# Four transformer layers on one core: plain float32 matmuls in place of three products of 12-bit parts

## The chip, the core and the metric

The kernel runs on one core of a Trainium2 chip. The metric is the device time of one execution in microseconds (us). The engines of the core are named as in the profile: PE is the tensor engine (PEld its weight loads), DVE the vector engine, ACT the scalar engine, POOL GpSimd, SP the engine whose queue issues most transfers. Each engine works through its own list of instructions in order and waits on semaphores.

## What is computed

One inference step of a diffusion backbone with 1024 features, for 512 latent tokens and 128 prompt tokens, 640 in all. There are four layers, each with another kind of attention over 16 heads (neighbourhood attention; a sliding window with grouped keys; latent attention of low rank with a rotary part; grouped keys with rotary positions). Everything is float32.

```python
for li in range(DEPTH):                                  # DEPTH = 4
    hp = modulate(rms_norm(xp, norm1_g[li]), mp[0], mp[1])   # prompt, 128 tokens
    hs = modulate(rms_norm(xs, norm1_g[li]), ms[0], ms[1])   # latents, 512 tokens
    ...                                                  # q, k, v; softmax(q k + bias) v; w_o
    x = x + gate * heads_out(o, w_o)
    h = modulate(rms_norm(x, norm2_g[li]), ...)
    x = x + gate * ((silu(h @ w_gate) * (h @ w_up)) @ w_down)   # 2816 hidden features
```

## The kernel before

A layer L has two stages. The attention stage makes the normalised and modulated activations (`make_h`), then the token-major products for queries, keys and values (`proj_first`, `proj`; for layer 2 `products_q` and `products_k`), normalises the heads, transposes queries and keys on PE, and goes through 16 units, each a pair of heads and a half of the latents: scores into PSUM tiles `S`, softmax, transposes of the weights into `tp`, the product with the values into `sm` (tiles `pt` and `v`). Between these, generators of other work are advanced a step at a time (`job`, `tick`): the next group's products, its preparation, a half of the output product, the next layer's modulation. The feed-forward stage (`rest`) finishes the output product, normalises again (`make_b`), and forms gate and up with seven block products in place of eight (`gate_up`: quarters of the weights and of the activations, and sums of such quarters named S1 to S4 and T1 to T4), then the product down. Feature-major products have 320 columns (half of the 640 tokens) and accumulate in tiles `big`.

Every linear product is made from parts: a float32 block of weights `raw` or `sum` is copied to a 12-bit high part `whi` on ACT (line 309, type float32r), and the rest `wlo` is the difference, on DVE or POOL (line 310). Activations are cut likewise into `hh` and `hl`, attention outputs and hidden features into `ah` and `al`. A product is then three matmuls: high by high, high by low, low by high (`mm3`, `feat`, `block`; all matmuls are recorded at line 269, in `mm`).

Scores use the array's 128 rows for 64 features: a head's queries stand as high part above low part (`stack`), its keys' high part is doubled into both halves of the rows, and so is the low part (`double`, by a transfer); two matmuls give the score, in layer 2 a third one adds the rotary part (tiles `qpe`, `kpe`).

The order of the instructions on each engine comes from a scheduler that a model of the time drives; blocks of attention have priority. Weight blocks have 4 places each for `raw`, `whi` and `wlo`, in the feed-forward stage 4, 9 and 9, and 4 for `sum`.

Some products are plain float32 already: the sums of squares against ones (tiles `t` and `consts`), the modulation (`raw`, `rawm` with `cond`, four products of 32 columns side by side in the array), the product with the values (two heads of 64 columns side by side).

Of the kernel before, what the change touches and what calls it, by code (L numbers as in the profile page):

```python
# [9 lines left out]
F32R = mybir.dt.float32r  # L10
# [4 lines left out]
P = 128  # L15
D = 1024
ND = 8
# [27 lines left out]
# ---------------------------------------------------------------- layout of the weights  # L45
# [5 lines left out]
def weight_plan():  # L51
    """(key, features tiles, columns, builder) of every weight of a product, in the order of use."""
# [59 lines left out]
# columns (one value a partition) and rows (one value a column, the same in every partition)  # L112
# [55 lines left out]
def to_perm(a):  # L168
    """Latent tokens from (row, column) order to (column // 8, row, column % 8) order, first axis."""
    return a.reshape(8, 8, 8, *a.shape[1:]).swapaxes(0, 1).reshape(a.shape)  # L170


def host_arrays(a):
# [54 lines left out]
    h["ck0"] = kdup(a["cache_na_k"], np.arange(HD))  # L228
# [31 lines left out]
# ---------------------------------------------------------------- the kernel  # L260
class Net:
    def __init__(self, nc, tc, a, o, depth=DEPTH):
        self.nc, self.tc, self.a, self.o, self.depth = nc, tc, a, o, depth
        self.flip, self.flop = 0, 0
        self.slots(None)

    # -- small helpers
# [3 lines left out]
    def alt(self, out, in_, share=0.5):  # L271
        """A copy, on the scalar engine for a share of the calls and on the vector engine for the others."""
        self.flip += share
        if self.flip >= 1:
            self.flip -= 1
            self.nc.scalar.copy(out, in_)
        else:
            self.nc.vector.tensor_copy(out, in_)

    def banks(self, kind):  # L280
        """The accumulators of a phase: name -> (banks of each, number)."""
# [8 lines left out]
    def weights(self, key, part=None):  # L290
        """The blocks of a weight, or one of them, on chip in two parts: for each feature tile (high, low) [128, n]."""
        i, k, n, per = WIDX[key]
        nc, out = self.nc, []
        for j, k0 in enumerate(range(0, k, per)):
# [4 lines left out]
            nc.sync.dma_start(raw[:, :w], self.a["wall"][i + j, :, :w])  # L299
            self.flop += 0 if self.more else 1  # L300
# [12 lines left out]
    def slots(self, more):  # L313
        """The places of blocks and of their parts, in turn; the feed-forward phase has some more of them."""
        self.more = more
        self.free = {n: [f"{n}{i}" for i in range(SLOTS)] for n in ("raw", "whi", "wlo")}
# [4 lines left out]
    def slot(self, name):  # L321
# [3 lines left out]
        return pool.tile([P, BLK], F32 if name in ("raw", "sum") else F32R, tag=tag, name=name)  # L325
# [12 lines left out]
    # -- the whole  # L338
# [38 lines left out]
    # -- modulation: silu(cond) @ w_mod + b_mod, as columns  # L377
# [6 lines left out]
    def mod_first(self, b, pool):  # L384
        """The first layer's shift and scale of feature tiles 2 b and 2 b + 1."""
# [22 lines left out]
    def mod_part(self, L, c0, w, pool, tag=None, bufs=1):  # L408
        """Columns c0 to c0 + 4 w - 1 of the layer's modulation: four products side by side in the array."""
# [32 lines left out]
    def fill(self, n):  # L442
        """n steps of the work that waits for idle time of the tensor engine."""
# [46 lines left out]
    def new_act(self):  # L490
        hi = self.cp.tile([P, T], F32R, tag="hh", name="hh", bufs=ND)
        lo = self.cp.tile([P, T], F32R, tag="hl", name="hl", bufs=ND)
        return hi, lo

    def make_h(self, pool, L, n, ds=range(ND), src=None):
# [3 lines left out]
        for d in ds:  # L499
            hi, lo = self.new_act()  # L500
            u = pool.tile([P, T], F32, tag="u", name="u", bufs=2)
            for c, (c0, c1) in enumerate(((0, NL), (NL, T))):
                s = src[d] if src is not None and c == 0 else self.x[:, d, c0:c1]
                nc.vector.scalar_tensor_tensor(u[:, c0:c1], s, moda[:, n, d, c:c + 1], self.rstd[:, c0:c1],
                                               ALU.mult, ALU.mult)
            for c, (c0, c1) in enumerate(((0, NL), (NL, T))):
                nc.scalar.activation(hi[:, c0:c1], u[:, c0:c1], AF.Identity, bias=self.mcol(L, 3 * n, d, c))
            for c, (c0, c1) in enumerate(((0, NL), (NL, T))):
                nc.vector.scalar_tensor_tensor(lo[:, c0:c1], u[:, c0:c1], self.mcol(L, 3 * n, d, c),
                                               hi.bitcast(F32)[:, c0:c1], ALU.add, ALU.subtract)  # L510
            self.h.append((hi, lo))

    # -- products
    def mm3(self, out, x, w, start, stop):
        """out += x.T @ w to float32's accuracy, from parts of 12 bits."""
        self.mm(out, x[0], w[0], start, False)
        self.mm(out, x[0], w[1], False, False)
        self.mm(out, x[1], w[0], False, stop)

    def proj_first(self, key, n, evac):  # L520
        """Token-major product of h, the features outermost: five accumulators of n columns."""
# [5 lines left out]
        for k, w in enumerate(self.weights(key)):  # L527
            hh, hl = self.h[k]
            for t in range(NTT):
                ts = slice(t * P, (t + 1) * P)  # L530
                self.mm3(acc[t], (hh[:, ts], hl[:, ts]), w, k == 0, k == ND - 1)
# [3 lines left out]
    def proj(self, key, n, evac):  # L535
        """Token-major product of h, a step for each tile of tokens."""
        ws = self.weights(key)
        for t in range(NTT):
            ts = slice(t * P, (t + 1) * P)
            acc = self.ps()[:, :n]  # L540
            for k in range(ND):
                hh, hl = self.h[k]
                self.mm3(acc, (hh[:, ts], hl[:, ts]), ws[k], k == 0, k == ND - 1)
# [28 lines left out]
    def residual(self, L, i, d, halves):  # L572
        """x += gate * y for one feature tile of y, or a half of it: halves is {half: y}."""
# [6 lines left out]
    # -- products by seven block products (Strassen, Winograd's form)  # L580
# [3 lines left out]
    def scaled(self, pool, L, halves, d, raws):  # L584
        """A feature tile of x (or a half of it) by its scale, for make_b."""
        nc = self.nc
        if d not in raws:
            raws[d] = pool.tile([P, T], F32, tag="a", name="raw", bufs=12)
# [10 lines left out]
    def make_b(self, pool, L, B, raws):  # L599
        """The second normalisation: the quarters of h that the seven block products take and their sums, all in two  # L600
        parts: B[name] = [(high, low) of feature tile i of the half's four]. A step for each feature tile of the first
        half of the tokens, and one for the rest. The latents' shift joins the quarters and sums when they are split."""
        nc = self.nc
        lo, hi = slice(0, 320), slice(320, T)
        t3 = [pool.tile([P, 2, 320], F32, tag="a", name="raw", bufs=12) for _ in range(HALF // 2)]
        slots = [self.new_act() for _ in range(ND)]
        for tag, w in (("c", T), ("d", 320)):
            slots += [[pool.tile([P, w], F32R, tag=x + tag, name=x, bufs=HALF) for x in ("hh", "hl")] for _ in range(HALF)]
        shift = self.mods[L][0][:, 24:24 + ND]
        more = pool.tile([P, ND + HALF], F32, tag="more", name="more")  # L610
        self.sub(nc.gpsimd, more[:, :ND], shift[:, :, 1], shift[:, :, 0])
        self.sub(nc.gpsimd, more[:, ND:], shift[:, HALF:, 0], shift[:, :HALF, 0])

        done = []
# [1118 lines left out]
```

## Time and profile before

| | |
|---|---|
| time, median of 3 runs | 3288.86 us (3283.66 to 3291.21) |
| span of the profiled execution | 3285.3 us |
| busy: PE, PEld, DVE, ACT, POOL | 3123.6, 2847.0, 2155.9, 1527.9, 1264.1 us |
| matmul records | 22157 |
| mean granted clock of PE | 0.979 of 2.4 GHz |

The span runs from the first to the last instruction of one profiled execution; for it no other time than the span is at hand, and it lies within the runs'. Busy time is the union of an engine's instructions. The chip records a plain float32 matmul as two instructions and one of type float32r as one; both are shown as f32.

### The profile page before, as it was taken

Reading aid. Unit: us, or ns where it says so; the run is one execution under the profiler, and the core shown is the slowest. Engines: PE = TensorE matmul, PEld = TensorE weight load, DVE = VectorE, ACT = ScalarE, POOL = GpSimd, SP = SyncE. Lnnn points to the kernel's source line nnn. Section 1 sums busy time; section 2 is a strip of 40 time slices with the busy share of each in tenths; the row PEclk is TensorE's granted clock in tenths of the full one; section 3 lists DMA queues with packets and bytes.
Section 4 is the critical chain, followed back from the end, with each engine's and each line's share of the span. In section 5 each row is a group of like instructions: output and inputs, shape, how many; then the busy total and the mean of one; then the engine's idle time right before and its main releaser. Section 6 shows DMA issues by size and latency. Waiting matters only on the chain. (4 is left out here: it accounts for less than half of the span.)

```text
span 3285.3 us, 58663 instructions
## 1 busy us (share of the span) xinstructions
PE 3123.6 (95%) x22157; PEld 2847.0 (87%) x22157; DVE 2155.9 (66%) x4167; ACT 1527.9 (47%) x3300; POOL 1264.1 (38%) x1175
## 2 busy tenths in 40 slices
PE   8999989999999999999987999999999999899999
PEld 6997879999887788999976778899998878799999
DVE  5554496666576768667668766865765765867665
ACT  4555453433346755334346765433433576534332
POOL 2442362322244444323234545432322553633322
PEclk9998999999999999999998999999999999899999
DMA  7346542433433343222211223423333111122222
GB/s 236 100 119 195 184 155 86 127 104 117 126 122 98 105 135 105 76 84 83 88 45 40 64 64 120 135 86 119 117 102 122 53 32 29 55 87 76 80 82 83
DMA packets 168251, 331.50 MB, mean 101 GB/s; under 512 B 19616, under 2 KB 49696, under 8 KB 167968
## 3 DMA queue, kind: packets, MB, share of 16 engines
q1 hardware_dynamic: 164800, 323.47, 32.6%
q8 instruction: 175, 2.87, 0.4%
q10 hardware_dynamic: 3168, 4.28, 0.4%
q14 instruction: 108, 0.88, 0.1%
HBM read 303.86 MB, written 4.28 MB: 94 GB/s over the span
## 5 line engine op out<-in xcount | busy, mean ns | idle before, releaser
L269 PE MATMUL big<-hh,whi 128*128 128x320 f32 x2720 | 829.9, 315 | 24.7 <-ACT hh L619 8.5
L269 PE MATMUL big<-hl,whi 128*128 128x320 f32 x2720 | 832.1, 312 | 6.7 <-DVE hl L623 4.6
L269 PE MATMUL big<-hh,wlo 128*128 128x320 f32 x2720 | 824.1, 311 | 0.9 <-DVE wlo L310 0.9
L309 ACT CAST whi<-raw 128x512 fp32r<-128x512 f32 (+3 forms) x668 | 387.7, 586 | 674.1 <-PE big L269 431.8
L310 DVE TENSOR_TENSOR wlo<-raw,whi 128x512 fp32r<-128x512 f32 (+1 forms) x504 | 432.5, 862 | 201.6 <-ACT whi L309 198.5
L269 PEld LDWEIGHTS big<-hh,whi 128*128 128x128 f32 x2720 | 508.4, 190 | 53.9 <-DVE sv L696 13.6
L269 PEld LDWEIGHTS big<-hl,whi 128*128 128x128 f32 x2720 | 511.7, 190 | 20.9 <-DVE hl L623 10.8
L269 PEld LDWEIGHTS big<-hh,wlo 128*128 128x128 f32 x2720 | 510.1, 189 | 2.9 <-DVE wlo L310 2.9
L310 DVE TENSOR_TENSOR wlo<-sum,whi 128x512 fp32r<-128x512 f32 x336 | 302.0, 903 | 73.3 <-ACT whi L309 68.4
L309 ACT CAST whi<-sum 128x512 fp32r<-128x512 f32 x352 | 215.8, 618 | 272.5 <-PE big L269 226.4
L269 PE MATMUL big<-al,whi 128*128 128x320 f32 x1408 | 335.9, 311 | 3.2 <-POOL al L582 3.2
L310 POOL TENSOR_TENSOR wlo<-raw,whi 128x512 fp32r<-128x512 f32 (+2 forms) x164 | 223.4, 1374 | 294.4 <-ACT whi L309 266.5
L269 PE MATMUL big<-ah,whi 128*128 128x320 f32 x1408 | 333.8, 312 | 1.2 <-ACT ah L734 1.2
L269 PE MATMUL big<-ah,wlo 128*128 128x320 f32 x1408 | 333.4, 310 | 0.0
L1018 POOL TENSOR_SCALAR p<-p,st 128x640 f32<-128x640 f32 (+2 forms) x256 | 201.2, 790 | 315.7 <-DVE st L1017 227.9
L709 POOL TENSOR_TENSOR y<-y,sv 128x320 f32<-128x320 f32 x132 | 146.7, 1118 | 354.0 <-DVE sv L696 300.8
L670 POOL TENSOR_TENSOR sum<-raw,sum 128x512 f32<-128x512 f32 x88 | 124.0, 1409 | 410.1 <-ACT whi L309 206.2
L670 POOL TENSOR_TENSOR sum<-raw 128x512 f32<-128x512 f32 x88 | 127.5, 1449 | 364.7 <-DMA raw<-in_wall 180.6
L577 DVE SCALAR_TENSOR_TENSOR x<-big,mod,x 128x320 f32<-128x320 f32 (+2 forms) x480 | 182.4, 432 | 117.4 <-PE big L269 116.8
L269 PEld LDWEIGHTS big<-al,whi 128*128 128x128 f32 x1408 | 240.2, 189 | 6.5 <-POOL al L582 3.7
L269 PEld LDWEIGHTS big<-ah,whi 128*128 128x128 f32 x1408 | 238.3, 188 | 8.0 <-issue 2.5
L269 PEld LDWEIGHTS big<-ah,wlo 128*128 128x128 f32 x1408 | 239.6, 189 | 0.2
(264 smaller groups left out, 6169.2 us busy)
## 6 DMA issues: line engine op xcount, KB each, us to landing
raw<-in_wall SPq DMA_DIRECT2D x644, 256.0 KB, 2.7
rawm<-in_wmod SPq DMA_DIRECT2D x144, 512.0 KB, 4.3
raw<-in_wmod SPq DMA_DIRECT2D x96, 256.0 KB, 4.5
k<-k SPq DMA_DIRECT2D x38, 384.0 KB, 4.4
raw<-in_wall SPq DMA_DIRECT2D x96, 128.0 KB, 2.2
bias<-in_nabias SPq DMA_DIRECT2D x16, 576.0 KB, 5.5
qpe<-pes SPq DMA_DIRECT2D x56, 80.0 KB, 2.1
out_y<-x ACTq DMA_DIRECT2D x8, 320.0 KB, 2.2
```

The source lines that it names most:

```text
L269: self.nc.tensor.matmul(out, lhsT=lhsT, rhs=rhs, start=start, stop=stop, skip_group_check=True)
L309: self.nc.scalar.copy(hi, raw)
L310: eng.tensor_tensor(lo, raw, hi.bitcast(F32), ALU.subtract)
L577: self.last = self.nc.vector.scalar_tensor_tensor(xs, halves[b][:, p0:p1], self.mcol(L, i, d, c), xs, ALU.mult, ALU.add)
L670: eng.tensor_tensor(raw[n], raw[x], raw[y], op)
L709: nc.gpsimd.tensor_tensor(y, y, v, ALU.mult)
L1018: nc.gpsimd.tensor_scalar(p, p, rd, 1.0, ALU.mult, ALU.mult)
```

## The change

All cuts into parts go, and with them `two`, `stack`, `split`, `double`, `o_split`, `acts`, `first_group` and `spread`. A linear product is one plain float32 matmul on the block and the activation as they are. A pair of heads has one tile of queries and one of keys, 64 rows for each head (where four heads share a key it stands in both halves, doubled before the transpose); a score is one matmul on 64 rows, and in layer 2 a second one on the 32 rows of the rotary part. Weight blocks get 12 places, in the feed-forward stage 20, sums 8. In `make_b` the normalised quarters are used in place and the sums are made from them. Attention outputs get tiles of their own (`oo`).

```diff
-SLOTS = 4
-MORE = {"whi": 5, "wlo": 5, "sum": 4}
+SLOTS = 12
+MORE = {"raw": 8, "sum": 8}
...
-            hi, lo = self.two(raw[:, :w], nc.gpsimd if self.flop >= 1 else nc.vector)
-            self.flop -= self.flop >= 1
-            out += [(hi[:, c:c + n], lo[:, c:c + n]) for c in range(0, w, n)]
+            out += [raw[:, c:c + n] for c in range(0, w, n)]
...
-    def two(self, raw, eng):
-        """The two parts of a block."""
-        hi, lo = (self.slot(n)[:, :raw.shape[1]] for n in ("whi", "wlo"))
-        self.nc.scalar.copy(hi, raw)
-        eng.tensor_tensor(lo, raw, hi.bitcast(F32), ALU.subtract)
-        return hi, lo
...
-    def mm3(self, out, x, w, start, stop):
-        """out += x.T @ w to float32's accuracy, from parts of 12 bits."""
-        self.mm(out, x[0], w[0], start, False)
-        self.mm(out, x[0], w[1], False, False)
-        self.mm(out, x[1], w[0], False, stop)
...
-        for k, ((wh, wl), (ah, al)) in enumerate(zip(ws, acts)):
-            for w, x, st, sp in ((wh, ah, k == 0, False), (wh, al, False, False), (wl, ah, False, k == n - 1)):
-                for b, bank in halves.items():
-                    self.mm(bank, w, x[:, COLS[b][0]:COLS[b][1]], st, sp)
+        for k, (w, x) in enumerate(zip(ws, acts)):
+            for b, bank in halves.items():
+                self.mm(bank, w, x[:, COLS[b][0]:COLS[b][1]], k == 0, k == n - 1)
...
+        def normal(d, c):
+            nc.vector.tensor_tensor(raws[d][:, c], raws[d][:, c], self.rstd[:, c], ALU.mult)
+            for k, (c0, c1) in enumerate(((0, NL), (NL, T))):
+                c0, c1 = max(c0, c.start), min(c1, c.stop)
+                if c0 < c1:
+                    nc.scalar.activation(raws[d][:, c0:c1], raws[d][:, c0:c1], AF.Identity,
+                                         bias=self.mcol(L, 3, d, k))
...
-    def block(self, out, A, B, start, stop, eng=None):
+    def block(self, out, A, B, start, stop):
 
-        h, l = self.two(A, eng or self.nc.vector)
-        for k, (xh, xl) in enumerate(B):
-            c = slice(k * P, (k + 1) * P)
-            self.mm(out, h[:, c], xh, start and k == 0, False)
-            self.mm(out, h[:, c], xl, False, False)
-            self.mm(out, l[:, c], xh, False, stop and k == len(B) - 1)
+        for k, x in enumerate(B):
+            self.mm(out, A[:, k * P:(k + 1) * P], x, start and k == 0, stop and k == len(B) - 1)
...
-    def score(self, out, q, k, qpe, kpe):
-        net = self.net
-        net.mm(out, q, k[:, 0], True, False)
-        net.mm(out, q, k[:, 1], False, False)
-        net.mm(out, qpe, kpe, False, True)
+    def score(self, h, out, c, k0, k1):
+        q, k = self.hd[h // 2]
+        r, rp = slice(h % 2 * 64, h % 2 * 64 + 64), slice(h % 4 * 32, h % 4 * 32 + 32)
+        self.net.mm(out, q[r, c], k[r, k0:k1], True, False)
+        self.net.mm(out, self.pe[h // 4][rp, c], self.kpe[rp, k0:k1], False, True)
```

The scheduler makes a new order of it. Three places follow. In a row stand the line, the operation, the tile written, the tiles read and the size of what is written.

On PE in a feed-forward stage, among the block products (`big`) with a step of modulation (`sm<-rawm,cond`) between them, before:

```order
L269 MATMUL big<-hh,whi 128x320
L269 MATMUL sm<-rawm,cond 32x256 x4
L269 MATMUL big<-hl,whi 128x320
L269 MATMUL big<-hh,wlo 128x320
L269 MATMUL big<-hh,whi 128x320
L269 MATMUL big<-hl,whi 128x320
```

and after:

```order
L268 MATMUL big<-hh,raw 128x320 x4
L268 MATMUL sm<-rawm,cond 32x256 x4
L268 MATMUL big<-sumb,sum 128x320 x8
L268 MATMUL sm<-rawm,cond 32x256 x4
L268 MATMUL big<-sumb,sum 128x320 x4
```

The triples on parts have become single products on the blocks (`raw`, `sum`) and on the activations and their sums (`hh`, `sumb`).

On PE in layer 2, a head's scores (`S`), the product with the values (`sm<-pt,v`) and transposes (`tp`), before:

```order
L269 MATMUL S<-k,qn 128x320 x2
L269 MATMUL S<-kpe,qpe 128x320
L269 MATMUL S<-k,qn 128x320 x2
L269 MATMUL S<-kpe,qpe 128x320
L269 MATMUL sm<-pt,v 64x256 x2
L986 MATMUL tp<-consts,qs 128x128
```

and after:

```order
L268 MATMUL S<-k,qn 128x320
L268 MATMUL S<-kpe,pes 128x320
L268 MATMUL S<-k,qn 128x320
L268 MATMUL S<-kpe,pes 128x320
L268 MATMUL sm<-pt,v 64x256 x10
L906 MATMUL tp<-consts,p 128x128 x8
```

Two records and a third, all on 128 rows, have become two products on 64 and on 32 rows, which alternate.

On DVE at the start of the last feed-forward stage, behind the residual of the output product: the multiplication by `rstd` (line 630, after the change 586), the low parts of the activations (`hl`) and of the weights (`wlo`), before:

```order
L630 TENSOR_TENSOR raw<-raw,rstd 128x320 x2
L670 TENSOR_TENSOR sum<-sum,raw 128x512
L623 SCALAR_TENSOR_TENSOR hl<-raw,mod,hh 128x320
L630 TENSOR_TENSOR raw<-raw,rstd 128x320
L623 SCALAR_TENSOR_TENSOR hl<-raw,mod,hh 128x320
```

and after:

```order
L554 SCALAR_TENSOR_TENSOR x<-big,mod,x 128x192
L554 SCALAR_TENSOR_TENSOR x<-big,mod,x 128x128
L586 TENSOR_TENSOR hh<-hh,rstd 128x320 x16
L559 TENSOR_TENSOR sumb<-hh 128x320 x2
L605 TENSOR_TENSOR sumb<-sumb,hh 128x320 x2
```

Multiplications that alternated with differences now stand in one row, and only the sums of quarters follow.

## Rows read from the trace of the kernel before

**Rows 1.** The page's first lines, and the core's mean granted clock.

```profile
span 3285.3 us, 58663 instructions
PE 3123.6 (95%) x22157; PEld 2847.0 (87%) x22157; DVE 2155.9 (66%) x4167; ACT 1527.9 (47%) x3300; POOL 1264.1 (38%) x1175
...
core 0: 3285.3 us, clock 0.979
```

**Rows 2.** Chain of waits, layer 3's two stages: start us, us, what, records.

```profile
2914.01 229.83 PE big L269 x1565
...
2529.55 2.72 PE S L269 x12
```

**Rows 3.** Windows around stage starts: stretch, length, engines' busy us, PEclk, DMA share, GB/s.

```profile
383.00:500.00 117.00, 106.77 (x769) 92.26 (x762) 96.26 (x156) 61.82 (x122) 65.78 (x49) 0.96 0.51 163
1175.00:1300.00 125.00, 116.08 (x807) 101.83 (x804) 102.12 (x167) 63.98 (x127) 70.03 (x53) 0.97 0.42 128
1995.00:2110.00 115.00, 106.43 (x764) 91.01 (x763) 94.44 (x156) 62.83 (x127) 67.24 (x53) 0.99 0.47 152
2785.00:2915.00 130.00, 113.03 (x689) 106.07 (x688) 104.30 (x164) 65.05 (x131) 72.80 (x54) 0.92 0.19 59
1682.00:1800.00 118.00, 92.94 (x484) 79.30 (x484) 94.84 (x235) 71.20 (x165) 55.51 (x64) 0.83 0.16 43
```

**Rows 4.** Timeline of PE, end of layer 3's output product: start us, us.

```profile
2825.24 0.31 PE L269 MATMUL big<-hh,wlo 128*128 128x320 f32 x1
2825.39 0.70 PE L269 MATMUL big<-t,consts 128*128 128x320 f32 x2
2825.68 0.55 PE L269 MATMUL big<-hh,whi 128*128 128x320 f32 x1
2826.07 0.31 PE L269 MATMUL big<-hl,whi 128*128 128x320 f32 x1
```

**Rows 5.** Tile t on PE: duration ns min/median/max, first and last start.

```profile
L269 PE MATMUL big<-t,consts x56: 431/433/537, 418.0 to 2828.7; 128*128 128x320 f32 x56
```

**Rows 6.** Groups of PE and PEld by shape, linear products: xcount | busy us, mean ns.

```profile
L269 PE MATMUL big<-hh,wlo 128*128 128x320 f32 x2720 | 824.1, 311 | 0.9 <-DVE wlo L310 0.9
L269 PE MATMUL big<-ah,whi 128*128 128x320 f32 x1408 | 333.8, 312 | 1.2 <-ACT ah L734 1.2
L269 PE MATMUL sm<-whi,hh 128*128 128x256 f32 x720 | 205.9, 291 | 1.2 <-DVE qs L278 1.2
L269 PE MATMUL sm<-hh,whi 128*128 128x320 f32 x256 | 84.5, 330 | 3.5 <-ACT whi L309 3.5
L269 PE MATMUL S<-whi,hh 128*128 128x512 f32 x82 | 32.7, 399 | 6.3 <-ACT hh L507 5.8 <-DVE qs L278 0.4
L269 PEld LDWEIGHTS big<-hh,whi 128*128 128x128 f32 x2720 | 508.4, 190 | 53.9 <-DVE sv L696 13.6 <-ACT hh L619 10.0 <-ACT hh L622 9.5
```

**Rows 7.** Groups of PE by shape, scores.

```profile
L269 PE MATMUL S<-k,qn 128*128 128x320 f32 x256 | 65.4, 338 | 7.7 <-ACT p L1008 2.8 <-ACT k L1655 2.4 <-ACT k L1656 1.0
L269 PE MATMUL S<-kpe,qpe 128*128 128x320 f32 x128 | 41.1, 321 | 0.0
L269 PE MATMUL S<-k,q 128*128 128x320 f32 x256 | 51.7, 326 | 5.1 <-ACT p L1008 3.8 <-DVE q L976 0.9
L269 PE MATMUL S<-k,q 128*128 128x128 f32 x352 | 63.9, 265 | 1.3 <-DVE st L1011 1.3
```

**Rows 8.** Timeline of PE around a step of modulation in layer 0's feed-forward stage.

```profile
590.98 0.31 PE L269 MATMUL big<-hh,wlo 128*128 128x320 f32 x1
591.22 1.07 PE L269 MATMUL sm<-rawm,cond 128*32 128x256 f32 x16
592.22 0.42 PE L269 MATMUL big<-hh,whi 128*128 128x320 f32 x1
592.47 0.31 PE L269 MATMUL big<-hl,whi 128*128 128x320 f32 x1
```

**Rows 9.** Timeline of PE in layer 3, scores of 128 columns.

```profile
2656.43 1.20 PE L269 MATMUL S<-k,q 128*128 128x128 f32 x8
2657.47 0.38 PE L986 MATMUL tp<-consts,p 128*128 128x128 f32 x2
```

More of the change, by code (lines that the diff above doesn't have):

```diff
@@ L269, in mm, with alt @@
         self.nc.tensor.matmul(out, lhsT=lhsT, rhs=rhs, start=start, stop=stop, skip_group_check=True)
-    def alt(self, out, in_, share=0.5):
+    def alt(self, out, in_, share=0.5, gain=None):
         self.flip += share
@@ L275, in alt @@
             self.flip -= 1
-            self.nc.scalar.copy(out, in_)
+            if gain is None:
+                self.nc.scalar.copy(out, in_)
+            else:
+                self.nc.scalar.activation(out, in_, AF.Copy, scale=gain)
+        elif gain is None:
+            self.nc.vector.tensor_copy(out, in_)
         else:
-            self.nc.vector.tensor_copy(out, in_)
+            self.nc.vector.tensor_scalar(out, in_, gain, None, ALU.mult)
     def banks(self, kind):
@@ L292, in weights @@
         i, k, n, per = WIDX[key]
-        nc, out = self.nc, []
+        out = []
         for j, k0 in enumerate(range(0, k, per)):
@@ L324, in slot @@
         pool = self.more if "_" in tag else self.wp
-        return pool.tile([P, BLK], F32 if name in ("raw", "sum") else F32R, tag=tag, name=name)
+        return pool.tile([P, BLK], F32, tag=tag, name=name)
     def row(self, name):
@@ L587, in scaled @@
         if d not in raws:
-            raws[d] = pool.tile([P, T], F32, tag="a", name="raw", bufs=12)
+            raws[d] = self.new_act()
         c0, c1 = COLS[halves[0]][0], COLS[halves[-1]][1]
@@ L604, in make_b @@
         lo, hi = slice(0, 320), slice(320, T)
[L605 to L611, printed above, removed]
@@ L612, in make_b @@
-        self.sub(nc.gpsimd, more[:, ND:], shift[:, HALF:, 0], shift[:, :HALF, 0])
-        done = []
-        def two(name, slot, c, x, bias=None, eng=nc.vector):
-            h, l = (y[:, c] for y in slots[slot])
-            if bias is None:
-                nc.scalar.copy(h, x)
-                done.append(self.sub(eng, l, x, h.bitcast(F32)))
-            else:
-                nc.scalar.activation(h, x, AF.Identity, bias=bias)
-                done.append(eng.scalar_tensor_tensor(l, x, bias, h.bitcast(F32), ALU.add, ALU.subtract))
-            B.setdefault(name, []).append((h, l))
@@ L626, in raw @@
-        def raw(d, c):
-            with contextlib.ExitStack() as st:
-                if len(done) >= 2:
-                    st.enter_context(self.tc.issue_after(done[-2].ins))
-                nc.vector.tensor_tensor(raws[d][:, c], raws[d][:, c], self.rstd[:, c], ALU.mult)
+        sums = {n: [pool.tile([P, 320], F32, tag=n, name="sumb", bufs=HALF) for _ in range(HALF)]
+                for n in ("T1", "T2", "T3", "T4")}
+        def normal(d, c):
[5 more added lines that the diff above has]
+                                         bias=self.mcol(L, 3, d, k))
@@ L632, in make_b @@
+        B.update(sums)
+        B["11"], B["21"] = ([raws[d][:, lo] for d in range(k, k + HALF)] for k in (0, HALF))
+        B["22"] = [raws[d][:, hi] for d in range(HALF, ND)]
         for d in range(ND):
-            raw(d, lo)
-            two(("11", "21")[d // HALF], d, lo, raws[d][:, lo], shift[:, d, 0:1])
+            normal(d, lo)
             yield
         for i in range(HALF):
-            for d in (i, i + HALF):
-                raw(d, hi)
-                p, m = raws[d][:, NL:], more[:, d:d + 1]
-                nc.scalar.activation(p, p, AF.Identity, bias=m)
@@ L650, in make_b @@
-        for i in range(HALF):
-            two("T3", ND + i, hi, t3[i // 2][:, i % 2], more[:, ND + i:ND + i + 1])
-        for i in range(HALF):
-            two("T4", ND + HALF + i, lo, raws[i + HALF][:, lo], eng=nc.gpsimd)
-        for i in range(HALF):
-            two("22", i + HALF, hi, raws[i + HALF][:, hi], shift[:, i + HALF, 0:1])
+            normal(i, hi)
+            self.sub(nc.vector, sums["T1"][i], raws[i][:, hi], raws[i][:, lo])
+            normal(i + HALF, hi)
+            self.sub(nc.gpsimd, sums["T3"][i], raws[i + HALF][:, hi], raws[i][:, hi])
@@ L656, in make_b @@
+        for i in range(HALF):
+            nc.vector.tensor_tensor(sums["T2"][i], sums["T3"][i], raws[i][:, lo], ALU.add)
+            self.sub(nc.gpsimd, sums["T4"][i], raws[i + HALF][:, lo], sums["T2"][i])
         yield
@@ L692, in gate_up @@
         if not up:
-            pair.extend(fp.tile([P, T], F32, tag="t", name="y", bufs=4) for _ in range(2))
+            pair.extend(fp.tile([P, T], F32, tag="y", name="y", bufs=12) for _ in range(2))
         def add(out, x, y):
@@ L730, in gate_up @@
         result(0, 1, d, v1)
-        if up:
-            for r in (1, 0):
-                hi, lo = (fp.tile([P, T], F32R, tag="a", name=n, bufs=12) for n in ("ah", "al"))
-                nc.scalar.copy(hi, pair[r])
-                self.sub(nc.gpsimd, lo, pair[r], hi.bitcast(F32))
-                pair[r] = (hi, lo)
         yield
@@ L964, in rope, with trs @@
         nc.vector.tensor_tensor(x, x, t2, ALU.add)
-    def stack(self, dst, rows, src, gain=None):
-        r = slice(rows, rows + 64)
-        self.split(dst[0:64], dst[64:128], src[r], None if gain is None else gain[r])
-    def split(self, hi, lo, src, gain=None):
-        nc = self.nc
-        if gain is None:
-            nc.scalar.copy(hi, src)
-            nc.vector.tensor_tensor(lo, src, hi.bitcast(F32), ALU.subtract)
-        else:
-            nc.scalar.activation(hi, src, AF.Copy, scale=gain)
-            nc.vector.scalar_tensor_tensor(lo, src, gain, hi.bitcast(F32), ALU.mult, ALU.subtract)
-    def double(self, t, r, o):
-        self.nc.sync.dma_start(t[o].bitcast(F32), t[r].bitcast(F32))
     def tr(self, out, in_):
         self.nc.tensor.transpose(out, in_, self.net.ident)
-    def trs(self, x, c, n):
-        out = self.tile([P, self.tiles * P], "trs", 2)[:, :n * P]
-        for t0 in range(0, n, 4):
-            t1 = min(t0 + 4, n)
-            tp = self.net.ps("tp")
+    def trs(self, x, c, outs, gain=None):
+        for t0, t1, out in outs:
+            tp = self.net.ps("tp")[:, :(t1 - t0) * P]
             for t in range(t0, t1):
                 self.tr(tp[:, (t - t0) * P:(t - t0 + 1) * P], x[:, t, c])
-            self.net.alt(out[:, t0 * P:t1 * P], tp[:, :(t1 - t0) * P])
-        return out
+            self.net.alt(out, tp, 0.5, gain)
     def softmax(self, s, w, bias=None, sink=None):
@@ L1037, in prompt @@
         w = n * P
-        s = net.ps("S")
-        s = (s[:, 0] if len(s.shape) == 3 else s)[:, :w]
+        if net.kind["S"][0] == 2:
+            both = net.ps("S")
+            s = [both[:, i, :P] for i in range(n)]
+        else:
+            s = [net.ps("S")[:, :P] for _ in range(n)]
         for i in range(n):
-            scores(i, s[:, i * P:(i + 1) * P])
+            scores(i, s[i])
         st = self.tile([P, 4, 4], "stp", 2)
         nm, den, rd, es = (st[:, i, :n] for i in range(4))
-        nc.vector.tensor_reduce(nm, s.rearrange("p (a b) -> p a b", a=n), axis=AX.X, op=ALU.max, negate=True)
+        for i in range(n):
+            nc.vector.tensor_reduce(nm[:, i:i + 1], s[i], axis=AX.X, op=ALU.max, negate=True)
         sink = self.sink
@@ L1156 @@
 class Mha:
-    pbufs, direct, tiles = 4, 5, NTT
+    pbufs = 4
     def body(self):
@@ L1182, in body @@
         self.units()
-        self.now(self.acts(8))
     def new_raw(self):
@@ L1203, in prep_q_pair, with scores @@
     def prep_q_pair(self, g, pr, gain):
-        tl = self.trs(self.raw["q", g], slice(pr * P, (pr + 1) * P), NTT)
-        for e in range(2):
-            q = self.tile([P, T], "q", 4, F32R)
-            yield
-            self.stack(q, 64 * e, tl, gain)
-            self.hd[4 * g + 2 * pr + e] = q
+        q = self.tile([P, T], "q", 3)
+        self.trs(self.raw["q", g], slice(pr * P, (pr + 1) * P), [(0, 4, q[:, :NL]), (4, 5, q[:, NL:])], gain)
+        self.hd[2 * g + pr] = q
         yield
-    def score(self, out, q, kh, kl):
-        self.net.mm(out, q, kh, True, False)
-        self.net.mm(out, q, kl, False, True)
     def prompt_group(self, g, pr):
-        i0 = 2 * pr
-        self.prompt(4 * g + i0, 2, lambda e, out: self.score(out, self.hd[4 * g + i0 + e][:, NL:],
-                                                             *self.kp(g, i0 + e)),
-                    lambda e: self.val(g, i0 + e, 5))
+        def scores(e, out):
+            r = slice(64 * e, 64 * e + 64)
+            self.net.mm(out, self.hd[2 * g + pr][r, NL:], self.kp(g, pr)[r], True, True)
+        self.prompt(4 * g + 2 * pr, 2, scores, lambda e: self.val(g, 2 * pr + e, 5))
 class Na(Mha, Attn):
-    rawbufs, nsteps, pg, pp = 4, 15, 14, 5
+    rawbufs, nsteps, pg, pp = 4, 15, 14, 2
     win = ((0, (0, 1)), (64, (6, 7)), (192, (7, 8)), (256, (2, 3)))
@@ L1337 @@
 class Gqa(Mha):
-    rawbufs, nsteps, pg, pp = 3, 5, 10, 3
+    rawbufs, nsteps, pg, pp = 3, 5, 9, 1
     def setup(self):
@@ L1452, in scores @@
     def scores(self, h, out, j, k0, k1):
-        k = self.kg[h // 4]
-        self.score(out, self.hd[h][:, j * P:(j + 1) * P], k[:, 0, k0:k1], k[:, 1, k0:k1])
+        r = slice(h % 2 * 64, h % 2 * 64 + 64)
+        self.net.mm(out, self.hd[h // 2][r, j * P:(j + 1) * P], self.kg[h // 4][r, k0:k1], True, True)
 class Mla(Full):
-    pbufs, direct, tiles = 4, 0, 6
+    pbufs = 4
     def body(self):
         pool, net = self.ap, self.net
-        self.kpe = self.tile([P, 768], "kpe", 1, F32R)
-        self.cc = self.tile([P, 2, P], "ckvc", 1, F32R)
+        self.kpe = self.tile([P, 768], "kpe")
+        self.cc = net.load("ckvc", [P, P], net.a["ckvT"], pool)
         self.qtab_tile = self.tile([P, NTT, 64], "qtab")
@@ L1701, in scores @@
     def scores(self, h, out, j, k0, k1):
-        q, k, qpe = self.hd[h]
-        c = slice(j * P, (j + 1) * P)
-        self.score(out, q[:, c], k[:, :, k0:k1], qpe[:, c], self.kpe[:, k0:k1])
+        self.score(h, out, slice(j * P, (j + 1) * P), k0, k1)
     def prompt_group(self, g, pr):
-        def scores(e, out):
-            q, k, qpe = self.hd[4 * g + 2 * pr + e]
-            self.score(out, q[:, NL:], k[:, :, T:], qpe[:, NL:], self.kpe[:, T:])
-        self.prompt(4 * g + 2 * pr, 2, scores, lambda e: self.val(g, 2 * pr + e, 5))
+        h0 = 4 * g + 2 * pr
@@ L1713, in build @@
+        self.prompt(h0, 2, lambda e, out: self.score(h0 + e, out, slice(NL, T), T, 768),
+                    lambda e: self.val(g, 2 * pr + e, 5))
 def build(h, depth=DEPTH):
```

280 lines of the change are left out of this document (70 added, 210 removed).

## The prediction

> **What bounds the kernel now.** I read the page first. The tensor engine is busy 3123.6 of 3285.3 us, 95%, the vector engine 66%, the scalar engine 47% [rows 1]. A busy share alone says little, because matmuls are pipelined and their recorded ends overlap the next start, so I went on to the chain of waits. In the last feed-forward stage it is one unbroken run of matmuls: 1565 records in 229.83 us, or 146.9 ns from start to start [rows 2]. There nothing but the tensor engine's own rate sets the end; the other engines follow. The windows around the starts of the four feed-forward stages and of layer 2 show the exceptions: there the tensor engine's busy time is 9 to 25 us under the window's length and the granted clock falls to 0.83 to 0.99 [rows 3]. So the question is what the new products cost the tensor engine, and how much of the waiting the removed preparation gives back.
>
> **Price of a product before.** A product of 320 columns on 12-bit parts is three records of 146.9 ns, 0.441 us [rows 2]. A 512-column one is 2.72 us / 12 = 0.2267 us a record, 0.680 us for three (the second row of [rows 2]). The line through both is 13.9 ns plus 0.416 ns a column; by it a 256-column record costs 0.120 us, three 0.361 us (an estimate from these two rows).
>
> **Price of a product after.** Before has plain float32 matmuls of the same shape: the sums of squares against ones (tiles t and consts), 56 records for 28 products, so two records each. In the timeline one such product starts at 2825.39, one cut product follows, and the next one starts at 2826.07: 0.68 us, less 0.147 for the cut one, leaves 0.53 us [rows 4]. The durations agree: a cut record lasts 311 ns on average [rows 6] and starts every 147, so 164 ns of it overlap the next; the plain record's median of 433 [rows 5] less 164 is 269 ns, two make 0.538 us. I take 0.538 for 320 columns, and in proportion 0.430 for 256 and 0.861 for 512. A weight load lasts 190 ns [rows 6], less than 269, and stays hidden.
>
> **Linear products.** Three records become two longer ones. The counts are the products with the high parts [rows 6]: 2720 + 1408 + 256 = 4384 of 320 columns, 4384 x (0.538 - 0.441) = 425 us. 720 of 256 columns, 720 x 0.069 = 50 us. Of 512 columns the row shows 82, the other accumulators in the same view add 62: 144 x 0.181 = 26 us. 80 more of 384 or 416 columns add 10. Together **+511 us**. The bounds are narrow, since the same operation at the same shape is in the trace: with 0.53 in place of 0.538 it is 35 us less.
>
> **Scores.** Before, layer 2 has 256 + 128 and layer 3 256 records of 320 columns, 640 x 0.147 = 94 us; the 128-column ones, 400 with the two small groups, take 1.04 us / 8 = 0.13 us each [rows 7, 9], 52 us; 192 of 256 and 64 of 384 columns make 34. Sum 180 us. After, by the program lists: 384 products of 320 columns (0.538), 96 of 256 (0.430), 32 of 384 (0.645) and 208 of 128 (0.215), sum 313 us. **+133 us** if each occupies the engine for its whole time. They use only 64 or 32 rows, and what that changes no row shows: above, they cost what full ones do; below, two heads' products overlap completely and it is 313 / 2 - 180 = -23. I take the upper end, because in the program's order the products of the two heads rarely stand next to each other: a head's blocks of keys come first, then its transposes.
>
> **Changes of shape in the array.** Where before turns from 128x128 products to four 32-column ones and back, time is lost: from 590.98 to 592.47 are 1.49 us, and the work in it is two cut records (0.294) and 16 plain records of 256 columns, four side by side (4 x 0.215), 1.15 us [rows 8]. So a round trip costs 0.34 us, a change 0.17. Counted in the programs' lists, neighbours of different shape number 675 before and 1279 after, mostly in layer 2 (87 to 426), where 64-row and 32-row score products alternate. 604 more at 0.17 make **+103 us**. No row has a change by rows rather than columns, so the bounds are 0 and 0.17 each; I take the dear end, the only one a row shows. The Trainium skill, TensorEngine Tiling, Key Properties, says that changing the tiling mode drains the engine. By that rule the 0.34 us is no accident of this place, and layer 2's alternating products could not overlap at all; the trace's column changes agree, its row changes are not there to ask. By the rule as by the row, the sum keeps the 103 us.
>
> **What comes back.** The casts to high parts and the subtractions for low parts (L309, L310, L582, L619 to L623) go, and with them their place in the chain. In the four feed-forward windows the idle time is 10.2 + 8.9 + 8.6 + 17.0 = 45 us, and the lower clock costs (1 - 0.96) x 117 + (1 - 0.97) x 125 + (1 - 0.99) x 115 + (1 - 0.92) x 130 = 20 us [rows 3]. There the vector engine has a multiplication and a subtraction for every tile; afterwards it has 16 multiplications and 8 sums, so I give back two thirds, 43 us. Outside, the recorded idle time is 3285.3 - 3123.6 - 45 = 117 us, and the clock's mean of 0.979 [rows 1] costs 69 us, 49 of them elsewhere. The first 13 us and the waits for modulation weights stay; a quarter of the idle time and half of the clock make 53 us. Sum **-96 us**. Bounds: 0, where every wait finds a new cause, and -231, where all of it goes. The copies of keys that now come from a doubled tile, the prompt's separate reductions and the wider query tiles cost scalar and vector time only; the cover is the lengthened matmul stream, on engines that are idle half of the time.
>
> Sum: 3285.3 + 511 + 133 + 103 - 96 = 3936 us. The profiled execution's 3285.3 lies 3.6 under the median 3288.86 of the runs, which I carry over: **3940 us**, 20% slower.
>
> **Rivals.** *The rows of the array are shared.* If all score products of two heads ran side by side, and changes of row shape cost nothing, 156 + 103 us would go: 3680 us; if a third of this holds, 3850. For it: the four 32-column products of a modulation step do run side by side [rows 8]. Against: the order of the program. The Trainium skill, TensorE: Matmul & The Clock Gate, Part 3, states that matmuls in different row groups run concurrently, which is this rival; no row here has such a pair. *The waits stay.* Layer 2's start loses its special path for the first two heads: the whole group is now normalised, its keys on GpSimd, before any score. That window already has 25 us of idle time and a clock of 0.83 [rows 3]. If nothing comes back and this start grows by half of its loss, (25 + 20) / 2 = 22 us, it is 3940 + 96 + 22 = 4058 us. *Faster than before.* If in a long stream a plain record costs only its weight load, 190 ns instead of 269 [rows 6], then the new products (4384 x 0.538 + 720 x 0.430 + 144 x 0.861 + 80 x 0.67 + 313 = 3160 us) shrink to 2232 and the kernel ends at 3012 us. The break-even is a record of 0.269 x (3160 - 651) / 3160 = 0.214 us. Against it stand the 56 records, none shorter than 431 ns [rows 5], that is 267 from start to start.
>
> **Chances.** The forecast with its own bounds, 3850 to 4020: 0.68. Shared rows, or more given back than I count, 3680 to 3850: 0.16. Waits that stay, over 4020: 0.12. Faster: 0.02; by a happy balance no change: 0.01; some other way to be slower: 0.01. The range that leaves out no more than two in ten is **3800 to 4050**: it takes in the third of the first rival and most of the second. A measurement of this kernel can tell about 0.2%, 7 us, from no change; slower holds 0.97, same 0.01, faster 0.02.
>
> **What would show it.** In the profile after, the feed-forward stages should be unbroken rows of plain matmuls, 269 ns from record to record, with two records a product, 0.97 busy or more, each of the four near 600 us. Layer 2 should be the stage with the largest share of lost time; a round trip out of the 64-row shape should cost 0.3 us. The vector engine should fall below half of the span. Wrong would be the forecast if records start every 215 ns or less, if the first product after a row change starts without delay, or if stalls at the stage starts grow.

## The result, and the profile after

The changed kernel takes 3988.85 us (median of 4 runs, 3988.68 to 3996.35) against 3286.73 for the kernel before (median of 4 runs); the ratio is 1.2143 (95% interval 1.2119 to 1.2168). The forecast was 3940, range 3800 to 4050.

The page after, the lines that answer to [rows 1], and the two of the tensor engine's busy share and granted clock in 40 slices:

```profile
span 3986.9 us, 44106 instructions
PE 3926.6 (98%) x16968; PEld 2585.2 (65%) x16968; DVE 1250.8 (31%) x3002; ACT 777.6 (20%) x1952; POOL 752.3 (19%) x878
...
PE   8999999999999999999899999999999999999999
...
PEclk9999999999999999999967788999999999999999
```

Fewer records, all engines but one with less to do, and a longer span. The tensor engine's idle time is 3986.9 - 3926.6 = 60 us where it was 162 [rows 1]. The odd place is in slices 21 to 25 of the second row: there the engine is busy, yet its granted clock reads 6 to 8 tenths.

The longest piece of the chain of waits, which answers to the first row of [rows 2]:

```profile
3465.62 517.05 PE big L268 x1920
```

It is 269.3 ns a record, two records a product: 0.539 us, to be compared with three of 146.9.

The windows by stage, from layer 1's feed-forward stage on (columns as in [rows 3]):

```profile
1341.30:1921.50 580.20, 575.15 (x2218) 399.42 (x2216) 162.73 (x330) 60.88 (x132) 105.34 (x96) 1.00 0.25 78
1921.50:2475.40 553.90, 541.20 (x1729) 266.81 (x1729) 172.99 (x456) 152.34 (x375) 102.66 (x153) 0.78 0.05 14
2475.40:3078.60 603.20, 597.76 (x2490) 405.33 (x2489) 168.35 (x345) 62.10 (x135) 104.80 (x96) 1.00 0.32 104
3078.60:3420.80 342.20, 338.72 (x1565) 212.77 (x1565) 136.65 (x308) 134.41 (x322) 85.01 (x110) 0.97 0.09 28
3420.80:3986.90 566.10, 558.77 (x2073) 393.30 (x2072) 157.33 (x318) 49.51 (x111) 107.35 (x97) 1.00 0.20 64
```

The same stretch of layer 2's attention in the kernel before, a row not shown so far:

```profile
1682.50:2004.00 321.50, 283.42 (x1757) 231.30 (x1757) 226.43 (x527) 201.69 (x464) 146.04 (x183) 0.93 0.21 55
```

The feed-forward stages have become what was forecast: 5 to 7 us of idle time each, full clock. Layer 2's attention stands out. It goes from 321.5 to 553.9 us, a third of the whole loss, and the granted clock in it is 0.78. By that share (1 - 0.78) x 553.9 = 122 us were lost to the low level of 1.2 GHz, 23 before.

The timeline of a block of scores there at the full clock (granted 1.00 from 2088.4 to 2091.3 us), and of a part of another at the low one (0.50 from 2012 to 2019); `x2` are the two records of one product:

```profile
2088.39 0.80 PE L268 MATMUL S<-k,qn 64*128 64x320 f32 x2
2089.12 0.80 PE L268 MATMUL S<-kpe,pes 32*128 32x320 f32 x2
2089.85 0.80 PE L268 MATMUL S<-k,qn 64*128 64x320 f32 x2
2090.58 0.80 PE L268 MATMUL S<-kpe,pes 32*128 32x320 f32 x2
2091.31 0.65 PE L268 MATMUL sm<-pt,v 128*64 128x256 f32 x4
...
2013.00 1.43 PE L268 MATMUL S<-kpe,pes 32*128 32x320 f32 x2
2014.36 1.43 PE L268 MATMUL S<-k,qn 64*128 64x320 f32 x2
```

A product of two records takes 0.73 us from start to start, though two records are 0.539: each change between 64 and 32 rows costs 0.19 us, and the two shapes do not overlap. At the low clock the same product takes 1.36 us.

Elsewhere two heads do overlap. In layer 0 there are eight records in a row, four of 256 columns and four of 128. The timeline names the first shape only; the last line, the view of the tile `q` in this stretch, has both:

```profile
171.60 0.93 PE L268 MATMUL S<-k,q 64*128 64x256 f32 x8
172.46 0.33 PE L906 MATMUL tp<-consts,pp 128*128 128x128 f32 x1
...
L268 PE MATMUL S<-k,q x8: 269/324/480, 171.6 to 172.3; 64*128 64x256 f32 x4, 64*128 64x128 f32 x4
```

One after the other, at the forecast's prices, they would be 4 x 0.215 + 4 x 0.107 = 1.29 us; they take 0.86. Here the list has the two heads' products next to each other.

### The profile page after: what moved, and what is told of

Read it like the earlier page. It is cut to its first block, busy times and chain, and to the rows that moved or that the text cites. A ratio compares the mean times of both kernels' runs of the same rounds, so it can differ in the third digit from the quotient of the medians.

```text
span 3986.9 us, 44106 instructions
## 1 busy us (share of the span) xinstructions
PE 3926.6 (98%) x16968; PEld 2585.2 (65%) x16968; DVE 1250.8 (31%) x3002; ACT 777.6 (20%) x1952; POOL 752.3 (19%) x878
## 4 chain that ended last, share of the span: by engine, by line
PE 96%; DMA 2%; DVE 1%; ACT 0%; issue 0%; SPq 0%; DVEq 0%; ACTq 0%
PE big L268 56%; PE sm L268 20%; PE S L268 14%; PE tp L906 5%; DMA rawm<-in_wmod 1%; PE tp L268 1%; DMA raw<-in_wmod 1%; DMA raw<-in_wall 0%; DVE qs L874 0%; DVE hh L586 0%; DMA xperm<-in_xperm 0%; DVE ss L867 0%; ACT pt L276 0%; ACT p L925 0%; DVE st L924 0%
## 5 line engine op out<-in xcount | busy, mean ns | idle before, releaser
L268 PE MATMUL big<-y,raw 128*128 128x320 f32 x2816 | 766.7, 433 | 0.0
L268 PEld LDWEIGHTS big<-y,raw 128*128 128x128 f32 x2816 | 533.7, 190 | 225.6 <-issue 4.1
L268 PE MATMUL big<-sumb,sum 128*128 128x320 f32 x2112 | 604.9, 435 | 1.3 <-DVE sumb L559 1.3
L268 PEld LDWEIGHTS big<-sumb,sum 128*128 128x128 f32 x2112 | 397.2, 190 | 180.5 <-issue 19.9
L268 PE MATMUL big<-hh,raw 128*128 128x320 f32 x1408 | 416.0, 437 | 1.1 <-ACT hh L590 1.1
L268 PE MATMUL sm<-raw,hh 128*128 128x256 f32 (+2 forms) x1540 | 384.3, 400 | 0.6 <-ACT qs L276 0.6
L268 PEld LDWEIGHTS big<-hh,raw 128*128 128x128 f32 x1408 | 269.2, 192 | 115.9 <-issue 4.3
L268 PEld LDWEIGHTS sm<-raw,hh 128*128 128x128 f32 x1540 | 289.0, 194 | 56.9 <-issue 15.2
L268 PE MATMUL big<-sumb,raw 128*128 128x320 f32 x704 | 204.2, 433 | 0.0
L268 PE MATMUL big<-hh,sum 128*128 128x320 f32 x704 | 203.9, 432 | 0.0
```

The source lines that it names most:

```text
L268: self.nc.tensor.matmul(out, lhsT=lhsT, rhs=rhs, start=start, stop=stop, skip_group_check=True)
```

## The experiments

Theory A: the time is the tensor engine's, from two records of 269 ns a product, from changes of shape in the array, and in layer 2 from the lower clock. Its rivals: only the records count (B); the changes count, but the clock fell for another reason (C); or waits and the new order took the time.

**All 128 rows in every score.** In layer 2, and likewise in the other layers:

```diff
-        self.net.mm(out, q[r, c], k[r, k0:k1], True, False)
-        self.net.mm(out, self.pe[h // 4][rp, c], self.kpe[rp, k0:k1], False, True)
+        self.net.mm(out, q[:, c], k[:, k0:k1], True, False)
+        self.net.mm(out, self.pe[h // 4][:, c], self.kpe[:, k0:k1], False, True)
```

> The kernel after the change, but every score product takes all 128 rows of its tiles of queries and keys (rotary parts too). Left out: the separation of the heads, so the scores mix two or four heads; number, columns and records of all products stay. Neighbours of different shape in the tensor engine's list fall from 1279 to 672, in layer 2 from 426 to 95. Theory A (a change of shape costs 0.19 us by layer 2's rows after the change, and the granted clock falls in layer 2 because its score products use few rows): 607 x 0.19 = 115 us less for the changes, 100 us less for the clock, 3989 - 215 = 3774 us, granted clock of layer 2 near 1.00. Theory B (only the records count, 269 ns each): 3989 us, no difference. Theory C (the changes count, the clock falls for another reason, gaps between heads): 3874 us with the clock still near 0.78.

Measured: 3789.0 us, ratio 1.1531 (1.1507 to 1.1554), mean clock 0.995. Layer 2's attention:

```profile
1911.00:2295.20 384.20, 370.64 (x1728) 240.11 (x1728) 172.57 (x456) 151.37 (x375) 102.73 (x153) 0.98 0.07 20
```

Theory A's total was 15 us too low, but A stands against B and C: as many products with as many records run 200 us faster when they take the whole array, and the clock of layer 2 comes back. By the clocks, (1 - 0.963) x 3987 - (1 - 0.995) x 3787 = 129 us of it; what is left, 71 us for 607 changes, is 0.12 us each on average, net of the overlap of heads that this kernel gives up. This run takes away the narrow products and the changes of shape at once, so it does not tell which of the two lowers the clock.

**Is it few rows or the pauses that lower the clock?** The pauses are those of 0.19 us at changes of shape. Layer 2's two products both on the head's 64 rows (`rot64`), both on 32 rows (`rot32`), or as they are but the 64-row pair of a block ahead of the 32-row pair (`grouped`):

```diff
-        self.net.mm(out, self.pe[h // 4][rp, c], self.kpe[rp, k0:k1], False, True)
+        self.net.mm(out, self.pe[h // 4][r, c], self.kpe[r, k0:k1], False, True)
```

> The kernel after the change, but in layer 2 the rotary product takes the same 64 rows as the product before it, in place of 32, so that the two do not change the shape between them. Left out: the separation of the heads in the rotary part. Neighbours of different shape fall by 205, all in layer 2 (426 to 221). Theory A1 (the clock falls because few rows are used): 205 x 0.19 = 39 us less, clock of layer 2 still well under 0.9, 3950 us. Theory A2 (the clock falls because of the pauses at changes between 64 and 32 rows): also most of the 100 us of the clock comes back, 3850 to 3880 us, clock of layer 2 over 0.95.

```diff
-        self.net.mm(out, q[r, c], k[r, k0:k1], True, False)
+        self.net.mm(out, q[rp, c], k[rp, k0:k1], True, False)
```

> The kernel after the change, but in layer 2 both products of a score take the 32 rows of the rotary part: no change of shape between them, and fewer rows in use than after the change. Left out: half of a head's own features, in layer 2's scores. Neighbours of different shape 1279 to 1056. The run with both on 64 rows took 3836 us at a clock of 0.991. Theory A2 (the pauses at the changes between 64 and 32 rows lower the granted clock): 3830 to 3850 us here too, clock 0.985 or more. Theory A3 (the 32-row products lower it by using few rows): clock of layer 2 under 0.8 and 3940 us or more.

```diff
-                for half in range(2):
-                    self.scores(4 * g + 2 * pr + e, s[:, half, :320], 2 * hf + jj, half * 320, half * 320 + 320)
+                for part in range(self.parts):
+                    for half in range(2):
+                        self.scores(4 * g + 2 * pr + e, s[:, half, :320], 2 * hf + jj, half * 320, half * 320 + 320, part)
```

> The kernel after the change, but in layer 2 a block's two 64-row products come before its two 32-row products, where the scheduler leaves them together: neighbours of different shape in layer 2 426 to 309, in all 1279 to 1162; every product stays as it is, and so does the result. Price of the changes: 117 x 0.19 = 22 us, 3967 us. Theory A2 (the pauses lower the clock): fewer of them in a block give part of the 100 us of the clock back, 3900 to 3940 us. Theory A3 (few rows in use): 3967 us, clock as after the change.

Measured: `rot64` 3835.5 us, ratio 1.1672 (1.1644 to 1.1700); `rot32` 3865.3, 1.1750 (1.1713 to 1.1788); `grouped` 3923.2, 1.1921 (1.1887 to 1.1954). Layer 2's attention in the three, in this order:

```profile
1922.60:2314.60 392.00, 378.46 (x1729) 225.58 (x1729) 172.96 (x456) 151.01 (x375) 103.13 (x153) 0.97 0.06 19
...
1922.40:2346.30 423.90, 411.20 (x1728) 244.45 (x1728) 172.27 (x456) 151.39 (x375) 102.26 (x153) 0.87 0.06 17
...
1920.80:2418.80 498.00, 484.92 (x1728) 264.52 (x1728) 173.22 (x456) 152.04 (x375) 102.95 (x153) 0.82 0.05 15
```

Neither theory alone. With 64 rows and no change between the two products the clock is 0.97, close to the 0.98 of full rows: so 64 rows do little. With 32 rows and no such change it is 0.87: rows do count when they are so few. With both shapes and all changes it is 0.78, although only half of its score products take 32 rows; with fewer changes 0.82. So the changes with their pauses and the 32 rows both pull. `rot64` has the clock of theory A2 and came 15 us under its range; `rot32` missed both of its expectations and lies between them; `grouped` came where the pauses put it.

The clock's course says where each pulls. In the changed kernel and in all four runs it fell while the engine waited at the stage's start (in the changed kernel the engine is busy 30.0 of the 40 us from 1960 to 2000), and the runs differ in how it came back. Two stretches behind that wait, in the changed kernel, in `rot32` and in `rot64` (length, PE busy, granted clock, DMA share, GB/s):

```profile
1988.00:2055.00 67.00, 67.00 (x154) 0.59 0.00 0
2055.00:2475.40 420.40, 418.94 (x1407) 0.78 0.03 10
...
1988.00:2055.00 67.00, 67.00 (x183) 0.60 0.00 1
2055.00:2346.30 291.30, 289.83 (x1378) 0.92 0.05 14
...
1988.00:2055.00 67.00, 65.31 (x287) 0.94 0.01 5
2055.00:2314.60 259.60, 257.28 (x1275) 1.00 0.05 15
```

Right behind the wait 32 rows alone keep the clock as low as both shapes do (0.60 and 0.59). Later it is 0.92 with 32 rows alone, and 0.78 with both shapes, in a stretch in which the engine is hardly ever idle: there the changes pull more than the rows.

**Linear products alone.** The changed products, buffers and second normalisation, with the scores of before on cut operands:

```diff
-        q = self.tile([P, T], "q", 3)
-        self.trs(self.raw["q", g], slice(pr * P, (pr + 1) * P), [(0, 4, q[:, :NL]), (4, 5, q[:, NL:])], gain)
...
+            q = self.tile([P, T], "q", 4, F32R)
+            yield
+            self.stack(q, 64 * e, tl, gain)
...
-        self.net.mm(out, q[r, c], k[r, k0:k1], True, False)
-        self.net.mm(out, self.pe[h // 4][rp, c], self.kpe[rp, k0:k1], False, True)
+        net.mm(out, q, k[:, 0], True, False)
+        net.mm(out, q, k[:, 1], False, False)
+        net.mm(out, qpe, kpe, False, True)
```

> One part alone: the linear products plain as after the change, the attention scores on 12-bit parts and 128 rows as before. Theory A, from before: 3287 + 511 for the longer linear products - 100 of recovered idle time = 3698 us; from after: 3989 - 133 for scores - 608 x 0.19 = 115 for changes of shape - 100 for the clock = 3641 us; so 3640 to 3700. Rival (the time went to waits and to the order, not to the longer products): under 3450. Rival (scores on 64 and 32 rows cost nothing beside the linear products): over 3900.

Measured: 3713.6 us, ratio 1.1306 (1.1284 to 1.1328), 429 us over the kernel before and 14 over the range of theory A. The rivals of this run fall. Its page and its clock:

```profile
span 3709.7 us, 44385 instructions
PE 3605.4 (97%) x16829; PEld 2525.8 (68%) x16829; DVE 1349.7 (36%) x3118; ACT 862.6 (23%) x2094; POOL 770.4 (21%) x883
...
core 0: 3709.7 us, clock 0.988
```

The tensor engine's idle time is 104 us where it was 162, and the clock costs 45 us where it cost 69: 58 and 24, together 82 us, came back. The spans differ by 424 us, so the longer records account for 506; the forecast had 511. And the scores, as changed, are the other 275 us of the whole change.

**One score product a head in layer 2.** The rotary queries are transposed into the free half of a head's rows (with 32 rows of zeros), the rotary keys copied beside the keys:

```diff
-        self.net.mm(out, q[r, c], k[r, k0:k1], True, False)
-        self.net.mm(out, self.pe[h // 4][rp, c], self.kpe[rp, k0:k1], False, True)
+        self.net.mm(out, q[:, c], k[:, k0:k1], True, True)
```

> The kernel after the change, but layer 2 has a tile of queries and one of keys for each head: 64 rows of the head's own part, 32 rows of the rotary part, 32 rows of zeros in the queries, so that a score is one product on 128 rows in place of two on 64 and 32. It takes 144 products less (128 of 320 columns, 16 of 128: 72 us) and some copies more on the other engines. Neighbours of different shape 1279 to 954, 62 us. Theory A: with the clock 3989 - 72 - 62 - 100 = 3755 us; without the clock's part 3855 us; if only records count 3917 us.

Measured: 3770.3 us, ratio 1.1473 (1.1456 to 1.1490). Layer 2's attention, 554 us after the change, takes

```profile
1919.70:2250.90 331.20, 305.40 (x1461) 190.02 (x1461) 186.45 (x488) 166.26 (x411) 118.61 (x169) 0.97 0.08 23
```

This is 10 us over the 321.5 of before. The total lies 15 us over that of theory A with the clock (3755), and 85 us under the next (3855).

**Two heads next to each other in the list.** On top of the last one, a pair's scores share one PSUM tile, so that nothing comes between them; here for layer 0; layer 1 has the like, and layer 3 a tile of four banks:

```diff
-                    s = net.ps("S")[:, :384]
-                    net.mm(s[:, :256], q, k[:, w0:w0 + 256], True, True)
-                    net.mm(s[:, 256:], q, k[:, T:], True, True)
+                    if e == 0:
+                        both = net.ps("S")
+                        for o, a, b in ((0, w0, w0 + 256), (256, T, 768)):
+                            for x in range(2):
+                                r = slice(64 * x, 64 * x + 64)
+                                net.mm(both[:, x, o:o + b - a], self.hd[2 * g + pr][r, j * P:(j + 1) * P], k[r, a:b], True, True)
+                    s = both[:, e, :384]
```

> The kernel with one score product on 128 rows in layer 2, and in the other layers the two heads of a pair share one PSUM tile for their scores, so that a product on rows 0 to 63 is followed at once by the other head's on rows 64 to 127. PSUM tiles of scores: in layers 0 and 1 two of two banks in place of three of one, in layer 3 one of four banks in place of two of two. Products of the two heads that stand next to each other: 61 before, 289 now; neighbours of different shape 954 to 827. If such products run side by side, 71 us less for them and 127 x 0.19 = 24 us for the changes: 3770 - 95 = 3675 us. If they do not: 3746 us. If the single large tile in layer 3 makes the tensor engine wait for the softmax: over 3770 us.

Measured: 3715.4 us, ratio 1.1296 (1.1272 to 1.1320): 55 of the 95 us. The timeline of two blocks in layer 3:

```profile
2984.55 1.35 PE L268 MATMUL S<-k,q 64*128 64x320 f32 x8
2985.83 0.33 PE L911 MATMUL tp<-consts,kd 128*128 128x128 f32 x1
...
3001.94 1.35 PE L268 MATMUL S<-k,q 64*128 64x320 f32 x8 [2.65 <-ACT p L930]
```

Eight records in 1.28 us, where one after the other they are 8 x 0.269 = 2.15: the heads do run side by side. The second block shows where some of the rest went: 2.65 us of waiting for the softmax (`p`) to free the one large tile. Layer 3's attention stage before and after the two heads share a tile:

```profile
2855.00:3196.90 341.90, 338.41 (x1565) 212.48 (x1565) 135.93 (x306) 134.22 (x321) 85.28 (x110) 0.97 0.09 28
...
2817.40:3147.00 329.60, 306.91 (x1565) 195.41 (x1565) 137.80 (x307) 134.37 (x322) 80.32 (x110) 0.97 0.10 31
```

The engine is busy 31.5 us less there, but idle 22.7 us in place of 3.5. These 19 us are about half of the 40 that are missing; the other half is not traced. This kernel is the fastest of the plain float32 kernels; none of the runs came under the kernel before.

## Why the prediction was right

The direction and the size were right, 49 us or 1.2% low. Step by step:

- *Price of a product after.* 0.538 us was read from 28 products; the stream of 1920 records gives 0.539. *Linear products*, +511: the run with these alone gives 506 by its idle time and clock.
- *Scores*, +133, was set at the full price. Between the linear products alone (3714) and all rows in use (3789) lie only 75 us, because this step takes away waits and clock loss too: layer 2 is busy 303.7 of 338.5 us with the cut scores (first line), and with all rows in use the engine is idle 62 us in the whole span, not 104, and the clock costs 19 us, not 45 (last two lines). The spans differ by 77 us; with 42 and 26 it is 145 for the records. Some 7 us of the difference to 133 are a misread row: the eight records behind the price of 0.13 us for 128 columns [rows 9] are four of 128 and four of 320 columns (second line), so a record of 128 columns is (1.04 - 4 x 0.147) / 4 = 0.113 us.

```profile
1902.80:2241.30 338.50, 303.73 (x1589) 207.46 (x1589) 204.94 (x492) 184.67 (x421) 114.85 (x158) 0.93 0.20 52
...
L269 PE MATMUL S<-k,q x8: 223/292/359, 2656.4 to 2657.3; 128*128 128x128 f32 x4, 128*128 128x320 f32 x4
...
PE 3724.9 (98%) x16968; PEld 2576.8 (68%) x16968; DVE 1254.0 (33%) x3002; ACT 777.1 (21%) x1952; POOL 749.9 (20%) x878
core 0: 3786.7 us, clock 0.995
```

- *Changes of shape in the array*, +103 at 0.17 us each: 71 us by the run with all rows, net of the heads' overlap, and 0.19 us each where 64 and 32 rows alternate. The dear end of the bounds was the right one in layer 2. The rule that a change of mode drains the engine (the Trainium skill, TensorEngine Tiling, Key Properties) agrees with these 0.19 us.
- *What comes back*, -96, is the term that was mis-sized. Its idle time came back more fully than I counted: 101 us, where the shares above come to 59. Its clock went the other way. I gave back 37 us of the clock's 69; it cost 147 after the change, 78 more, because layer 2's narrow products in alternating shapes lowered it to 0.78. The profile of before had no such products, but it did show that the clock falls where the engine is held up, and I counted their pauses only as time.

With the two prices of records as forecast and the other terms as measured the sum is 511 + 133 + 71 - 101 + 78 = 692 us, and the spans differ by 701.6. So the mechanism was right, but part of the closeness is luck: the clock was 115 us worse than forecast (37 given back, 78 lost), and against that stand 42 us more of idle time that came back and 32 us less for the changes of shape.

The first rival was half right. Two heads' products do run side by side, on rows 0 to 63 and 64 to 127, as the Trainium skill, TensorE: Matmul & The Clock Gate, Part 3, has it. Eight such records took 1.28 us in place of 2.15, but the scheduler's order left only 61 such neighbours in the changed kernel, and a change of row shape is not free (0.19 us). The second rival was wrong: layer 2's start lost its special path, yet the idle time of that whole stage fell from 38.1 to 12.7 us. The third needed records of 214 ns; they take 269.

What stays open: how much of the clock's loss in layer 2 is the 32 rows' and how much the pauses'. The runs show that both pull, and where, but do not divide the loss.

## What to carry to other kernels

Price a change of number format by the records it makes and the spacing of such records, not by the number of instructions: here the engine that set the end had 23% fewer records, and the kernel took 21% longer, because the two records of a plain product held the engine for 0.539 us where the three of a cut one held it for 0.441. Work removed from engines that are half idle gives back only the waits that they caused. When a product no longer fills the rows of the array, put the two that share it next to each other in the list, do not alternate shapes, and fill the rows if that saves a second product.

## What was not expected of the hardware

A tensor engine that is busy 541 of 554 us can still run at a granted clock of 0.78, when its score products alternate between 64 and 32 rows; with all of them on 64 rows it was 0.97, on 32 rows 0.87. In the changed kernel it fell in a wait of the engine and then stayed low or fell again in a stretch with hardly a wait (0.78 with the engine busy 419 of 420 us). A busy share does not show this, the clock's row does.
